# RWKV-7 time mixing in a two-layer decoder trunk: the keys as three split products, the gate's low-rank input mixed on VectorE

## The chip, the cores and the metric

The kernel runs on one core of a Trainium2 chip, in one launch. The metric is the device time of one execution in microseconds (us), as the median of several. A core has TensorE (PE; its weight loads are listed apart as PEld), VectorE (DVE), ScalarE (ACT), GpSimd (POOL) and SyncE (SP, which issues the loads here). Each engine works through a queue of its own in order, and waits for the others by semaphores.

## The reference, cut to what matters

The trunk has two layers over 256 tokens of width 1024. The first mixes tokens by RWKV-7 time mixing, the second by windowed attention; each layer has a half-step SwiGLU feed-forward net before and after the mixing. The change lies in the front of time mixing, where the projections are made:

```python
def rwkv7_time_mix(x, mu, w_rkv, w_o, w0, w1, w2, a0, a1, a2, g1, g2, ...):
    x_prev = jnp.pad(x, ((0, 0), (1, 0), (0, 0)))[:, :-1]
    xx = x_prev - x
    xr, xw, xk, xv, xa, xg = [x + xx * mu[i] for i in range(6)]
    r = xr @ w_rkv[0]
    k = xk @ w_rkv[1]                       # 256x1024 by 1024x1024
    v = xv @ w_rkv[2]
    w = -softplus(-(w0 + jnp.tanh(xw @ w1) @ w2)) - 0.5
    a = sigmoid(a0 + (xa @ a1) @ a2)
    g = sigmoid(xg @ g1) @ g2               # g1: 1024x128
    ...                                     # recurrence over tokens, normalization by head
    return (y * g) @ w_o
```

## The kernel before, in words

Everything is in float32, with tiles of 128 partitions; a width of 1024 is 8 chunks of 128 (KT), the tokens are two halves of 128 (`toks`). A float32 matmul takes two PE records for each call. Most of the large products avoid that: `mm3` (L180) and the feed-forward nets (L298, L299) split both operands into a high part, rounded to fp32r, and the low rest, and add three fp32r products, each one record: high by high, high by low, low by high. ACT casts the high part of a weight (L158, L141, `split` at L268), DVE subtracts for the low part (L164, L142, L269).

The front of time mixing does not split. In the order of the program it is:

- `tm_consts` (L442): during the feed-forward net ahead, loads the low-rank weights `lora1` and multiplies them by mu on DVE (L447), once for each of w1, a1 and g1, so that xw @ w1 = u @ w1 + xx @ (mu w1).
- `tm_in(i)` (L468), for each half of the tokens: normalizes, transposes (L263), scales into `uT` (ACT L479, DVE L482) and makes the difference `xx` (L488).
- `mix` (L459): u + xx mu for one of the inputs, 8 instructions on DVE (L456).
- `tm_lora(i)` (L509): 32 calls of 128x128x128 for one half, u and xx against both halves of `lora1` (L516); then tanh, copy and sigmoid on ACT (L518 to L520).
- `v_half` (L544): one half of tokens by 512 columns of w_v (L551).
- in `tm_core`: decay and gate of the low-rank inputs (L580, L586, L581, L588), cumulative decay by a matmul with a triangle (L595) and its exponentials on ACT into `Dp` and `Di` (L598, L599).
- K, in four steps p of 256 output columns: `k_mm(p)` (L637, by `feat_raw`) loads two raw weights of 128x1024 and issues 16 float32 matmuls of 256 columns (L506); `k_norm` squares, sums by head and scales (ACT L647, L649, L659, L661; PE L654; DVE L665, L666), `k_fin` transposes back (PE L677). `k_mm(1)` comes between `k_norm(0)` and `k_fin(0)`, and so on (L711 to L730). R follows the same way, by `feat_raw` (L690).

Raw weights lie in a pool of four buffers (`wr`), so a load on SP's queue (L123) starts when the user of the buffer four earlier is through. PSUM banks for these products are four.

Behind this come the inverses and the recurrence, in two halves of heads (`hh`) and two blocks of 64 tokens by halves. Its last part, where this document looks: `u_step` (L846 matmuls, L847 copies), `x_step` (L855 matmuls, L856 on DVE), what the state of the block before takes from the right-hand side `xtl` (L951 matmuls, L952 on DVE), the output sums (L865, L876), the normalization by head `gn_half` (L964 to L990, DVE L984 and L985), and `out_proj` (L994) with w_o split by L141 and L142, the transposed output by L268 and L269.

The order on each engine isn't the order of the code: the whole program is scheduled before it is built, from estimated durations, and the sequence for each engine's queue is fixed then. A change in one stage can so move instructions in another. The code's own dependences for order (`after`, `gate`, `behind`) hold in both versions.

Of the kernel before, what the change touches and what calls it, by code (L numbers as in the profile page):

```python
# [9 lines left out]
F32R = mybir.dt.float32r  # L10
AF = mybir.ActivationFunctionType
ALU = mybir.AluOpType
# [4 lines left out]
P = 128  # L17
D = 1024
T = 256
KT = 8  # L20
# [29 lines left out]
class Trunk:  # L50
# [129 lines left out]
    def mm3(self, out, l, r, first, last):  # L180
        mm = self.nc.tensor.matmul
# [259 lines left out]

    def tm_consts(self):  # L442
        nc = self.nc
        u, x = self.l1 = [self.tl("l1", [P, KT, 256], tag=f"l1{j}") for j in range(2)]
        self.load(u, self.a["lora1"].rearrange("p (k c) -> p k c", k=KT), self.mid)
        for j, c0, cw in ((1, 0, 64), (4, 64, 64), (5, 128, 128)):
            nc.vector.tensor_tensor(x[:, :, c0:c0 + cw], u[:, :, c0:c0 + cw],  # L447
                                    self.cols[:, C_MU + j * 8:C_MU + j * 8 + 8].unsqueeze(2).to_broadcast([P, KT, cw]),
                                    op=ALU.mult)
        nc.gpsimd.memset(self.hwa[64:65, 0, :], 1.0)  # L450
        nc.gpsimd.memset(self.hwa[0:64, 1, :], 0.0)
        nc.gpsimd.memset(self.hwa[0:1, 1, :], 1.0)
# [56 lines left out]
    def tm_lora(self, i):  # L509
        nc = self.nc  # L510
        sl = slice(i * P, (i + 1) * P)
        bs = [self.bank()[:, 0:P] for _ in range(2)]
        for e, (l, x) in enumerate(zip(self.l1, (self.uT, self.xx))):
            for j in range(2):
                for k in range(KT):
                    nc.tensor.matmul(bs[j], l[:, k, j * P:(j + 1) * P], x[:, k, sl], start=(k == 0 and not e),  # L516
                                     stop=(k == KT - 1 and e == 1))
        nc.scalar.activation(self.hwa[0:64, 0, sl], bs[0][0:64, :], AF.Tanh)  # L518
        nc.scalar.copy(self.hwa[64:128, 1, sl], bs[0][64:128, :])
        nc.scalar.activation(self.sgT[:, sl], bs[1], AF.Sigmoid)  # L520

    def tm_core(self):
        nc, a, DC = self.nc, self.a, self.DC
        mm = nc.tensor.matmul
        TT, STT = nc.vector.tensor_tensor, nc.vector.scalar_tensor_tensor
# [5 lines left out]
        toks = [slice(0, P), slice(P, T)]  # L531
# [5 lines left out]
        nc.vector.tensor_scalar(self.ka1, self.cols[:, C_KA:C_KA + KT], -1.0, 1.0, op0=ALU.mult, op1=ALU.add)  # L537
        nc.vector.tensor_scalar(self.nkk, self.cols[:, C_KK:C_KK + KT], -1.0, None, op0=ALU.mult)
        xv = self.tl("xt", [P, KT, P], tag="xv0")
        xk = self.tl("xt", [P, KT, T], tag="xtl")  # L540
        self.mix(xv, 3, toks[0])
        self.mix(xk[:, :, toks[0]], 2, toks[0])
        self.tm_lora(0)
        def v_half(n, x):  # L544
            acc = self.bank()
            ns = slice(n * 512, n * 512 + 512)
            for k2 in range(4):
                w = self.pp.tile([P, 2, 512], F32, name=f"wr{self.uid()}", tag="wr", bufs=4)
                self.load(w, a["w_v"][2 * k2:2 * k2 + 2, :, ns].rearrange("k p c -> p k c"))
                for k in range(2):  # L550
                    mm(acc, x[:, 2 * k2 + k, :], w[:, k, :], start=(k2 + k == 0), stop=(k2 + k == 4))  # L551
            return acc

        acc0 = v_half(0, xv)
        self.mix(xk[:, :, toks[1]], 2, toks[1])
        self.tm_lora(1)
        self.close("g2k", "t4", "W1", "W2", "l1")
        self.banks(4, 2)
# [1 line left out]
        self.open("GS")  # L560
        self.open("pk")
        self.open("ar", side="right")
        pk = lambda tag, shape, bufs=1: self.pools["pk"].tile(shape, F32, name=f"{tag}_{self.uid()}", tag=tag, bufs=bufs)
        vv = self.tl("el", [P, 2, D], tag="vv")
        v0 = vv[:, 0, 0:512]
# [9 lines left out]
        for i in range(2):  # L575
            sw.append(pk("p1", [P, D], 2))
            for n in range(2):
                ns = slice(n * 512, n * 512 + 512)
                b = self.bank()
                mm(b, self.hwa[0:65, 0, toks[i]], l2[0][0:65, ns], start=True, stop=True)  # L580
# [9 lines left out]
        for n in range(2):  # L590
            for i in range(2):
                b = self.bank()
# [12 lines left out]
        f = lambda ap: ap.rearrange("p s t -> p (s t)")  # L605
# [29 lines left out]
        kst = {}  # L635

        def k_mm(p):  # L637
            kst[p] = [self.feat_raw(a["w_k"], p, xk)]

        def k_norm(p):  # L640
            kb = kst[p][0]
# [158 lines left out]
        for s in range(31):  # L800
            n = 31 - s
# [20 lines left out]
        for hh in range(2):  # L822
            b = self.cbank()
            for v in range(16):
                for e in range(2):
                    mm(b[hi[e], v * 32:v * 32 + 32], ga(e, hh)[lo[e], v, 32:64], T1[lo[e], hh * 16 + v, :],
                       start=True, stop=True)
            for e in range(2):
                nc.scalar.copy(M1[hi[e], hh * 16:hh * 16 + 16, :], b[hi[e]].rearrange("p (v t) -> p v t", v=16))
        for hh in range(2):  # L830
            b = self.cbank()
            for v in range(16):
                for e in range(2):
                    mm(b[lo[e], v * 32:v * 32 + 32], M1[hi[e], hh * 16 + v, :], Wd[hi[e], hh * 16 + v, :],
                       start=True, stop=True)
# [62 lines left out]
        for e in range(2):  # L898
            for mq in range(2):
                b = self.tbank()  # L900
# [25 lines left out]
        y = [yy[:, 0], yy[:, 1]]  # L926
# [17 lines left out]
        for hh in range(2):  # L944
            s = slice(hh * 64, hh * 64 + 64)
            b = self.cbank()
# [365 lines left out]
```

## Time and profile before

| what | us |
|---|---|
| median of 3 runs | 1119.68 (1118.95 to 1120.72) |
| the profiled execution | 1121.3 |
| its span, first to last instruction | 1119.5 |
| PE busy in the span | 1087.2 (97%) |
| DVE busy | 684.0 (61%) |
| ACT busy | 547.1 (49%) |
| POOL busy | 66.5 (6%) |

So 1.8 us lie around the span, and the profiled execution is 1.6 us above the median. The granted clock of PE had a mean of 0.977 of full speed.

How to read the lines: in the timeline a row has the start, the duration, the engine, the line of the kernel, the operation, output and inputs by the program's names, the shape and, behind an x, how many instructions of a kind are merged; a bracket gives the idle time ahead of it and who ended it. PE's records overlap: a record is longer than the distance to the next one, so the rate is read from starts. In the table of windows a row has the stretch, its length, the busy time and count of PE, PEld, DVE, ACT and POOL, the granted clock, the busy share of the DMA engines and GB/s. In the groups by line, behind the bar stand the total busy time and the mean ns of one.

### The profile page before, as it was taken

The numbers are of one execution on the slowest core, as the hardware profiler recorded it, in microseconds if no ns is written. First come the engines' busy times: TensorE is split into PE (matmuls) and PEld (weight loads), VectorE is DVE, ScalarE is ACT, GpSimd is POOL, SyncE is SP. The second block draws the span as 40 slices with busy tenths as digits, with TensorE's granted clock in tenths as the row PEclk, the third lists the DMA queues.
The fourth block names the chain that finished last, engine by engine and source line by source line (L and its number), as shares of the span: only waits on it lengthen the run. The fifth ranks groups of instructions, "written<-read, shape, count | busy, mean of one in ns | idle before, by whom it ended". The sixth has DMA issues, their size and how long they took to land.

```text
span 1119.5 us, 16276 instructions
## 1 busy us (share of the span) xinstructions
PE 1087.2 (97%) x6360; PEld 895.8 (80%) x6360; DVE 684.0 (61%) x1076; ACT 547.1 (49%) x972; POOL 66.5 (6%) x68
## 2 busy tenths in 40 slices
PE   7999999999999999999999899999999899999997
PEld 5888888778777787888888678888887567888886
DVE  6666664615581677776565767656647756766652
ACT  6554553263322235665554546555535655655541
POOL 0000000000000000000000600000022421000000
PEclk9999999999987699999999999999999899999999
DMA  8767662223442332677665356665624324766521
GB/s 287 227 194 272 221 190 97 95 71 99 133 132 89 117 99 94 227 242 234 200 190 162 117 166 236 185 246 189 190 88 152 131 94 134 262 204 191 189 93 38
DMA packets 52957, 184.10 MB, mean 164 GB/s; under 512 B 5776, under 2 KB 6032, under 8 KB 52752
## 3 DMA queue, kind: packets, MB, share of 16 engines
q1 hardware_dynamic: 52592, 182.53, 50.1%
q8 instruction: 50, 0.82, 0.3%
q10 hardware_dynamic: 288, 0.52, 0.1%
q14 instruction: 27, 0.22, 0.1%
HBM read 181.98 MB, written 1.05 MB: 163 GB/s over the span
## 4 chain that ended last, share of the span: by engine, by line
PE 87%; issue 4%; DVE 4%; ACT 2%; DMA 2%; POOL 1%; SPq 0%; POOLq 0%; DVEq 0%; ACTq 0%
PE bt L298 12%; PE bk L298 12%; PE bk L182 11%; PE bk L186 11%; PE bk L187 11%; PE bk L299 6%; PE bt L299 6%; PE bk L506 5%; PE bk L551 3%; PE bt L616 2%; POOL W L162 1%; PE bt L625 1%; PE bt L263 1%; PE bc L846 1%; PE bk L876 1%
## 5 line engine op out<-in xcount | busy, mean ns | idle before, releaser
L164 DVE TENSOR_TENSOR W<-wr,W 128x1024 fp32r<-128x1024 f32 x267 | 327.9, 1234 | 192.3 <-ACT W L158 190.8
L158 ACT CAST W<-wr 128x1024 fp32r<-128x1024 f32 x284 | 296.3, 1050 | 210.7 <-issue 98.9
L186 PE MATMUL bk<-W,g2k 128*128 128x512 f32 x352 | 138.6, 394 | 0.0
L182 PE MATMUL bk<-W,g2k 128*128 128x512 f32 x352 | 138.5, 395 | 0.0
L187 PE MATMUL bk<-W,g2k 128*128 128x512 f32 x352 | 138.3, 394 | 0.0
L298 PE MATMUL bk<-xtl,W 128*128 128x512 f32 x296 | 105.2, 395 | 0.0
L298 PE MATMUL bt<-xtl,W 128*128 128x512 f32 x296 | 104.9, 394 | 0.0
L298 PE MATMUL bt<-xth,W 128*128 128x512 f32 x296 | 104.8, 393 | 0.0
L298 PE MATMUL bk<-xth,W 128*128 128x512 f32 x296 | 104.8, 393 | 0.0
L299 PE MATMUL bt<-xth,W 128*128 128x256 f32 x296 | 82.9, 280 | 0.0
L299 PE MATMUL bk<-xtl,W 128*128 128x256 f32 x296 | 82.9, 280 | 0.0
L299 PE MATMUL bt<-xtl,W 128*128 128x256 f32 x296 | 82.9, 281 | 0.0
L299 PE MATMUL bk<-xth,W 128*128 128x256 f32 x296 | 82.9, 280 | 0.0
L182 PEld LDWEIGHTS bk<-W,g2k 128*128 128x128 f32 x352 | 66.1, 188 | 15.6
L187 PEld LDWEIGHTS bk<-W,g2k 128*128 128x128 f32 x352 | 66.0, 188 | 15.7
L186 PEld LDWEIGHTS bk<-W,g2k 128*128 128x128 f32 x352 | 66.2, 188 | 14.2
L162 POOL TENSOR_TENSOR W<-wr,W 128x512 fp32r<-128x512 f32 x34 | 48.8, 1462 | 356.1 <-ACT W L158 356.1
L298 PEld LDWEIGHTS bk<-xth,W 128*128 128x128 f32 x296 | 55.6, 188 | 12.6
L298 PEld LDWEIGHTS bt<-xtl,W 128*128 128x128 f32 x296 | 55.6, 188 | 12.6
L298 PEld LDWEIGHTS bk<-xtl,W 128*128 128x128 f32 x296 | 55.6, 188 | 12.5
L298 PEld LDWEIGHTS bt<-xth,W 128*128 128x128 f32 x296 | 55.5, 188 | 12.5
L299 PEld LDWEIGHTS bk<-xtl,W 128*128 128x128 f32 x296 | 55.8, 188 | 1.3
(274 smaller groups left out, 1792.6 us busy)
## 6 DMA issues: line engine op xcount, KB each, us to landing
wr<-in_w_in_dram SPq DMA_DIRECT2D x148, 512.0 KB, 3.8
wr<-in_w_out_dram SPq DMA_DIRECT2D x88, 512.0 KB, 3.6
wr<-in_w_in_lead_dram SPq DMA_DIRECT2D x28, 512.0 KB, 3.9
wr<-in_w_v_dram SPq DMA_DIRECT2D x16, 512.0 KB, 3.9
gain<-in_rows_dram SPq DMA_DIRECT2D x15, 512.0 KB, 5.5
wr<-in_w_k_dram SPq DMA_DIRECT2D x8, 512.0 KB, 4.2
wr<-in_w_r_dram SPq DMA_DIRECT2D x8, 512.0 KB, 3.5
wr<-in_w_o_dram SPq DMA_DIRECT2D x8, 512.0 KB, 3.8
```

Of the source, the lines that this page charges most:

```text
L158: self.follow(nc.scalar.copy(w[:, 0, :], raw), 0)
L162: self.follow(nc.gpsimd.tensor_tensor(w[:, 1, ns], raw[:, ns], w[:, 0, ns], op=ALU.subtract), 2)
L164: self.follow(nc.vector.tensor_tensor(w[:, 1, :], raw, w[:, 0, :], op=ALU.subtract), 1)
L182: m = mm(out, l[0], r[0], start=first, stop=False)
L186: mm(out, l[0], r[1], start=False, stop=False)
L187: return mm(out, l[1], r[0], start=False, stop=last)
L263: t = self.nc.tensor.transpose(b[:, k * P:(k + 1) * P], xn[:, c:c + P], self.ident)
L298: mm(banks[j], hi[:, c0:c0 + P], xt[c][:, :, k4, :], start=(k == 0), stop=False)
L299: use[0] = mm(banks[j][:, 0:T], lo[:, c0:c0 + P], xt[c][:, 0, k4, :], start=False, stop=(k == KT - 1))
L506: mm(b[:, j * T:(j + 1) * T], ws[k // 4][:, c0:c0 + P], xf[:, k, :], start=(k == 0), stop=(k == KT - 1))
L551: mm(acc, x[:, 2 * k2 + k, :], w[:, k, :], start=(k2 + k == 0), stop=(k2 + k == 4))
L616: mm(bb[hh][:, (2 * x + sl) * N:(2 * x + sl + 1) * N], l, r, start=True, stop=True)
```

## The change

**The gate's low-rank input.** DVE mixes xg = u + xx mu (8 instructions for each half, into a tile of the pool `l1`), and `tm_lora` multiplies it once by g1: 8 calls fewer for each half. The product mu g1 in `tm_consts` goes.

**The keys.** The mixed xk goes to another tile, is cast to fp32r by ACT and its rest is made by DVE, for each half of the tokens. `k_mm` splits each raw weight in two halves of 512 columns (ACT L268, DVE L269) into one of three buffers of the new pool `kw`, and issues `mm3` of 256 columns: 48 products for each p, 192 in all, where 64 float32 calls with two records each were.

```diff
-        for j, c0, cw in ((1, 0, 64), (4, 64, 64), (5, 128, 128)):
+        for j, c0, cw in ((1, 0, 64), (4, 64, 64)):
...
         for e, (l, x) in enumerate(zip(self.l1, (self.uT, self.xx))):
-            for j in range(2):
-                for k in range(KT):
-                    nc.tensor.matmul(bs[j], l[:, k, j * P:(j + 1) * P], x[:, k, sl], start=(k == 0 and not e),
-                                     stop=(k == KT - 1 and e == 1))
+            for k in range(KT):
+                nc.tensor.matmul(bs[0], l[:, k, 0:P], x[:, k, sl], start=(k == 0 and not e),
+                                 stop=(k == KT - 1 and e == 1))
+        for k in range(KT):
+            nc.tensor.matmul(bs[1], self.l1[0][:, k, P:2 * P], self.xg[:, k, :], start=(k == 0), stop=(k == KT - 1))
...
-        xk = self.tl("xt", [P, KT, T], tag="xtl")
+        xkm = self.tl("xt", [P, KT, T], tag="xth")
+        xkh = self.tl("xt", [P, KT, T], F32R, tag="xtl")
+        def mix_g(i):
+            self.xg = self.tl("l1", [P, KT, P], tag="xg")
+            self.mix(self.xg, 5, toks[i])
+
+        mix_g(0)
         self.mix(xv, 3, toks[0])
-        self.mix(xk[:, :, toks[0]], 2, toks[0])
+        self.mix(xkm[:, :, toks[0]], 2, toks[0])
         self.tm_lora(0)
...
+        mix_g(1)
...
+        self.open("kw")
+        kw = lambda tag, shape, bufs: self.pools["kw"].tile(shape, F32R, name=f"{tag}_{self.uid()}", tag=tag, bufs=bufs)
+        xk = kw("xkl", [P, KT, T], 1)
+        for i in range(2):
+            self.nc.scalar.copy(xkh[:, :, toks[i]], xkm[:, :, toks[i]])
+            TT(xk[:, :, toks[i]], xkm[:, :, toks[i]], xkh[:, :, toks[i]], op=ALU.subtract)
...
         def k_mm(p):
-            kst[p] = [self.feat_raw(a["w_k"], p, xk)]
+            b = self.bank()
+            for c in range(2):
+                raw = self.raw(a["w_k"][2 * p + c])
+                for n in range(2):
+                    w = kw("wk", [P, 2, 512], 3)
+                    ns = slice(n * 512, n * 512 + 512)
+                    self.split(w[:, 0], w[:, 1], raw[:, ns])
+                    for j in range(2):
+                        for k2 in range(2):
+                            k = 4 * c + 2 * n + k2
+                            c0 = k2 * 256 + j * P
+                            self.mm3(b[:, j * T:(j + 1) * T], (w[:, 0, c0:c0 + P], w[:, 1, c0:c0 + P]),
+                                     (xkh[:, k, :], xk[:, k, :]), k + j == 0, k == KT - 1, skip_group_check=True)
+            kst[p] = [b]
...
-        self.close("pk")
+        self.close("kw", "pk")
```

The new code has 27 lines more by the end of `k_mm`, so the lines behind it are numbered higher: L647 becomes L674, L665 L692, L846 L873, L856 L883, L952 L979, L985 L1012. Between, L580 becomes L594, L595 L609, L598 L612, L762 L789.

**Where instructions moved.** Three places matter below. The first is ACT's queue between the low-rank products of the first half of tokens and those of the second, with the copies of `tm_in` for the second half (L479). `sgT` is the gate, `vv` the values, `wk` a half chunk of split keys' weights. Before:

```order
L519 COPY hwa<-bk_1799 64x128
L520 ACT_TABLE_LOAD
L520 ACTIVATE sgT<-bk_1800 128x128
L479 ACTIVATE u_94<-bt_1755,cols 128x128
L479 ACTIVATE u_94<-bt_1765,cols 128x128
L566 COPY vv_1926<-bk_1836 128x512
L479 ACTIVATE u_94<-bt_1755,cols 128x128
L479 ACTIVATE u_94<-bt_1765,cols 128x128
```

With the change:

```order
L520 COPY hwa<-bk_1808 64x128
L268 CAST wk_2014<-wr_2012 128x512
L521 ACT_TABLE_LOAD
L521 ACTIVATE sgT<-bk_1809 128x128
L268 CAST wk_2029<-wr_2012 128x512
L575 CAST xtl_1782<-xth_1781 128x8x128
L479 ACTIVATE u_94<-bt_1754,cols 128x128
L268 CAST wk_2046<-wr_2044 128x512
L479 ACTIVATE u_94<-bt_1764,cols 128x128
L479 ACTIVATE u_94<-bt_1754,cols 128x128
L580 COPY vv_1936<-bk_1837 128x512
L479 ACTIVATE u_94<-bt_1764,cols 128x128
```

Three casts of keys' weights, the first of which waits for its load, and the cast of the first half of xk now stand among the copies.

The second place is ACT's queue ahead of the exponentials. `p` are sigmoids of the decay, `av` those of the low-rank a, and L762 (L789) copies a part of `vv` whose mix stands late on DVE. Before:

```order
L581 ACTIVATE p_295_1935<-bk_1939 128x512
L762 COPY u_2421<-vv_1926 64x2x4x64
L762 COPY xx_2422<-vv_1926 64x2x4x64
L581 ACTIVATE p_298_1942<-bk_1943 128x512
L581 ACTIVATE p_298_1942<-bk_1946 128x512
L588 ACTIVATE av_1952<-bk_1949 128x512
L661 ACTIVATE p_321_2023<-av_1952,ka_77,cols 128x256 x2
L588 ACTIVATE av_1957<-bk_1954 128x512
L588 ACTIVATE av_1962<-bk_1959 128x512
L588 ACTIVATE av_1967<-bk_1964 128x512
L598 ACT_TABLE_LOAD
```

With the change:

```order
L595 ACTIVATE p_303_1952<-bk_1956 128x512
L602 ACTIVATE av_1962<-bk_1959 128x512
L688 ACTIVATE p_330_2077<-av_1962,ka_77,cols 128x256 x2
L602 ACTIVATE av_1967<-bk_1964 128x512
L789 COPY u_2608<-vv_1936 64x2x4x64
L789 COPY xx_2609<-vv_1936 64x2x4x64
L602 ACTIVATE av_1972<-bk_1969 128x512
L602 ACTIVATE av_1977<-bk_1974 128x512
L612 ACT_TABLE_LOAD
```

The two copies of `vv` moved from behind the second sigmoid to a place ahead of the last two, nearer to the table load.

The third place is DVE's queue at the end of the recurrence, in stages that the diff doesn't touch. `xtl` is the right-hand side that the products of `u_step` read, `xth` the output under normalization, `wo` the split output weight, `BK` the split output. Before:

```order
L984 TENSOR_TENSOR xth_3131<-xth_3131,gst_3390 128x8x64 x2
L952 TENSOR_TENSOR xtl_2427<-xtl_2427,bc_3244 128x8x64
L985 TENSOR_TENSOR xth_3131<-xth_3131 128x8x64 x2
L952 TENSOR_TENSOR xtl_2427<-xtl_2427,bc_3262 128x8x64
L142 TENSOR_TENSOR wo_3374<-wr_3375,wo_3374 128x1024
```

With the change:

```order
L1011 TENSOR_TENSOR xth_3318<-xth_3318,gst_3577 128x8x64 x2
L1012 TENSOR_TENSOR xth_3318<-xth_3318 128x8x64 x2
L979 TENSOR_TENSOR xtl_2614<-xtl_2614,bc_3431 128x8x64
L979 TENSOR_TENSOR xtl_2614<-xtl_2614,bc_3449 128x8x64
L142 TENSOR_TENSOR wo_3561<-wr_3562,wo_3561 128x1024
```

The first subtraction from `xtl` now stands behind both additions of L985 (now L1012). On ACT at the same place, one copy of `u_step` moved ahead of the casts of w_o; before:

```order
L982 ACTIVATE gst_3390<-gst_3390 128x8 x2
L141 CAST wo_3374<-wr_3375 128x1024
L141 CAST wo_3374<-wr_3379 128x1024
L847 COPY u_2421<-bc_3280 64x8x64
L268 CAST BK_3385<-bt_3414 128x4x128
```

With the change:

```order
L1009 ACTIVATE gst_3577<-gst_3577 128x8 x2
L874 COPY u_2608<-bc_3467 64x8x64
L141 CAST wo_3561<-wr_3562 128x1024
L141 CAST wo_3561<-wr_3566 128x1024
L874 COPY u_2608<-bc_3477 64x8x64
L268 CAST BK_3572<-bt_3601 128x4x128
```

The copy waits for products (L873) that read `xtl` after the first subtraction, so the casts behind it wait for them too.

More of the change, by code (lines that the diff above doesn't have):

```diff
@@ L178, in follow, with mm3 @@
             self.tc.add_manual_dep(ins.ins, self.behind[e], GATE, reason="order of the splits")
-    def mm3(self, out, l, r, first, last):
-        mm = self.nc.tensor.matmul
+    def mm3(self, out, l, r, first, last, **kw):
+        mm = lambda *x, **y: self.nc.tensor.matmul(*x, **y, **kw)
         m = mm(out, l[0], r[0], start=first, stop=False)
@@ L443, in tm_consts @@
         nc = self.nc
-        u, x = self.l1 = [self.tl("l1", [P, KT, 256], tag=f"l1{j}") for j in range(2)]
+        u, x = self.l1 = [self.tl("l1", [P, KT, 256 - 128 * j], tag=f"l1{j}") for j in range(2)]
         self.load(u, self.a["lora1"].rearrange("p (k c) -> p k c", k=KT), self.mid)
-        for j, c0, cw in ((1, 0, 64), (4, 64, 64), (5, 128, 128)):
+        for j, c0, cw in ((1, 0, 64), (4, 64, 64)):
             nc.vector.tensor_tensor(x[:, :, c0:c0 + cw], u[:, :, c0:c0 + cw],
@@ L554, in tm_core @@
         acc0 = v_half(0, xv)
-        self.mix(xk[:, :, toks[1]], 2, toks[1])
+        mix_g(1)
+        self.mix(xkm[:, :, toks[1]], 2, toks[1])
         self.tm_lora(1)
```

## The prediction

> **What bounds the kernel now.** I read the chain that ended last first, then the busy times by stretch of the front of time mixing (199 to 225 us the low-rank inputs, to 235 the gates, to 300 the keys and what follows).
>
> ```profile
> PE 87%; issue 4%; DVE 4%; ACT 2%; DMA 2%; POOL 1%; SPq 0%; POOLq 0%; DVEq 0%; ACTq 0%
> ```
> ```profile
> 199.00:225.00 26.00, 24.79 (x163) 19.59 (x162) 17.90 (x55) 8.12 (x24) 1.25 (x3) 1.00 0.31 102
> 225.00:235.00 10.00, 10.00 (x56) 7.82 (x54) 2.28 (x9) 8.73 (x15) 0.00 (x0) 1.00 0.16 52
> 235.00:300.00 65.00, 64.17 (x462) 52.80 (x462) 27.87 (x52) 24.41 (x55) 0.00 (x0) 1.00 0.37 114
> ```
>
> TensorE carries 87% of the chain. From 235 us on it is busy 64.2 of 65 us while VectorE and ScalarE have more than half of their time free: products removed there are time removed. The first two stretches look as full but aren't bound by PE: ScalarE has 8.7 of 10 us between 225 and 235, and the rows below show PE's starts hanging on copies and exponentials.
>
> **The front, up to the first key product.** PE's starts, then VectorE's, ScalarE's, and two prices from the page:
>
> ```profile
> 209.02 7.03 PE L551 MATMUL bk<-wr,xv 128*128 128x512 f32 x16
> ...
> 216.94 4.13 PE L516 MATMUL bk<-u,l 128*128 128x128 f32 x32
> 220.91 3.74 PE L516 MATMUL bk<-xx,l 128*128 128x128 f32 x32
> 224.48 3.60 PE L580 MATMUL bk<-gain,hwa 65*128 65x512 f32 x8
> ...
> 235.24 7.17 PE L506 MATMUL bk<-xtl,wr 128*128 128x256 f32 x32
> ```
> ```profile
> 204.63 1.13 DVE L456 SCALAR_TENSOR_TENSOR xv<-xx,cols,u 128x128 f32<-128x128 f32 x4
> ...
> 216.93 0.79 DVE L482 TENSOR_SCALAR u<-bt,cols 128x128 f32<-128x128 f32 x2 [7.21 <-ACT u L479]
> 218.11 0.61 DVE L482 TENSOR_SCALAR u<-bt,cols 128x128 f32<-128x128 f32 x2 [0.39 <-ACT u L479]
> ...
> 225.37 1.92 DVE L456 SCALAR_TENSOR_TENSOR vv<-xx,cols,u 128x128 f32<-128x128 f32 x7
> ```
> ```profile
> 209.73 0.28 ACT L520 ACTIVATE sgT<-bk 128x128 f32<-128x128 f32 x1
> 216.52 0.81 ACT L479 ACTIVATE u<-bt,cols 128x128 f32<-128x128 f32 x2 [6.51 <-PE bt L263]
> ...
> 232.81 1.28 ACT L598 ACT_TABLE_LOAD   x1
> ...
> 234.60 0.59 ACT L599 ACTIVATE Di<-bk 128x512 f32<-128x512 f32 x1
> ```
> ```profile
> L164 DVE TENSOR_TENSOR W<-wr,W 128x1024 fp32r<-128x1024 f32 x267 | 327.9, 1234 | 192.3 <-ACT W L158 190.8
> L158 ACT CAST W<-wr 128x1024 fp32r<-128x1024 f32 x284 | 296.3, 1050 | 210.7 <-issue 98.9
> ...
> wr<-in_w_k_dram SPq DMA_DIRECT2D x8, 512.0 KB, 4.2
> ```
>
> *The low-rank products.* 16 records fewer for each half, 32 in all, at 3.74/32 = 0.117 us: 3.74 us of PE. I book nothing for it. For the first half, PE waits afterwards for u of the second (u at 216.9); for the second, the 8 calls by xg must wait until VectorE has mixed it. The mix is 8 x 0.263 (1.05 us from one row's start to the next for four) = 2.1 us in each half, ahead of the other mixes. The multiplication of g1 that goes lies in the feed-forward net ahead, where it hid already.
>
> *What ScalarE and VectorE get more.* Two casts of xk (1.05 each) and two rests (1.23), and 16 half casts (0.53) and rests (0.62) of keys' weights. Three of the casts and one of xk stand among the copies of u. Their weight is loaded when `v_half` frees a buffer, after its second matmul: it starts some 1.9 before its old 209.0 (16 records fewer) and has four records at 0.44 (7.03/16) by then, so the load starts at 209 and lands 4.2 later, at 213. Then come cast 0.53 (half of 1.05, as a rest is half of 1.23), table load 1.28, gate 0.28, cast 0.53, cast of xk 1.05: the copy of u starts at 216.7, where it started at 216.5. On VectorE the rest of xk (1.23) stands ahead of the scaling of u, so it starts at 217.9 instead of 216.9, and the third cast stretches what follows: u is complete at 220.25 instead of 218.72 (1.5 late). xg is there at 225.1, and the decay (L580, now L594) starts at 225.45 instead of 224.48.
>
> *Up to the keys.* The last mixes end at 227.29 before (225.37 + 1.92). Added ahead of them are 1.5 of lateness, 2.1 of xg and 1.23 of the second rest of xk, less 0.4 of gaps that fill: 231.7. The copies of `vv` (L789) wait for these mixes, and in ScalarE's new order two sigmoids and the table load wait behind the copies: 231.85 + 1.24 for the copies + 1.0 for the sigmoids = 234.1, where the table load began at 232.81. The first product of K needs the bank that L599 reads last, so it follows that: 234.60 + 0.59 = 235.19 against the start at 235.24. Now it starts 1.25 later, at 236.5. **Term: +1.25**; from 0, if the copies are ready earlier, to +2.5, if the load of w_k lands a microsecond later and all stands behind it.
>
> **The keys.** A PE record of 512 and one of 256 columns in turn, from a feed-forward net, the weight loads of the second kind, the start of the second `v_half` behind K and R(0), and three prices of what stands between the casts:
>
> ```profile
> 104.22 0.40 PE L298 MATMUL bk<-xtl,W 128*128 128x512 f32 x1
> 104.45 0.28 PE L299 MATMUL bk<-xtl,W 128*128 128x256 f32 x1
> 104.58 0.39 PE L298 MATMUL bk<-xtl,W 128*128 128x512 f32 x1
> ...
> 107.00 0.39 PE L298 MATMUL bk<-xth,W 128*128 128x512 f32 x1
> ```
> ```profile
> L299 PEld LDWEIGHTS bk<-xtl,W 128*128 128x128 f32 x296 | 55.8, 188 | 1.3
> ```
> ```profile
> 284.66 0.65 PE L677 MATMUL bk<-cst,p 128*128 128x128 f32 x4
> 285.15 5.32 PE L551 MATMUL bk<-wr,xv 128*128 128x512 f32 x12
> ```
> ```profile
> L659 ACT ACTIVATE p<-rr 128x512 f32<-128x512 f32 x4 | 2.5, 628 | 18.0 <-DVE rr L657 18.0
> L661 ACT ACTIVATE p<-av,ka,cols 128x256 f32<-128x256 f32 x6 | 3.2, 586 | 0.0
> ```
>
> Before, K is 128 records at 7.17/32 = 0.224: 28.7 us. Now it is 192 products of 256 columns. Eight pairs of 512 and 256 take 107.00 - 104.22 = 2.78, 0.347 each; less 0.23 (104.22 to 104.45) leaves 0.117 for 256 columns. 192 x 0.117 = 22.5: **term -6.3**.
>
> No row shows 256-column fp32r passes alone, each with a new weight. The low bound is 0.117, as the float32 records of 128 columns above also come, a new weight each, at 0.117. The high bound is the 0.188 of a load's record, as if loads could not overlap: 36.1 us, +7.4. I take 0.117, since 0.347 for two passes is already less than two loads of 0.188. Beside it, the Trainium skill, page "TensorE: Matmul & The Clock Gate", section "The mechanism" of its Part 3, states that a weight load overlaps running matmuls only if its row group differs, and section "LDWEIGHTS (loading the stationary operand)" gives columns/1.2 ns, 107 ns for 128. By it I estimate 192 x (0.107 + 0.117) = 43 us, 14 more than K has now; the measured pair of 0.347 is below the 0.56 it would need, so the trace speaks against it.
>
> *Do the splits keep up?* A half chunk is 12 products, 1.40 us; its cast and rest, 0.53 and 0.62 on two engines, fit. The queue matters: three buffers let ScalarE run ahead by two half chunks, and in K(1) the ninth cast waits for the products of the sixth; behind it stand a table load (1.28), L659 (0.63) and two L661 (1.17), then the tenth cast (0.53) and its rest (0.62), 4.8 us with the ninth itself, in which PE has three half chunks, 4.2, and transposes of 0.5 (284.66 to 285.15). That leaves 0.1; VectorE, though, is then at products of k_norm and k_fin over 512 columns (0.68, as L952 below), of which two can stand ahead of the rest. I take 1.2 of idle PE there. **Term: +1.2**, from 0.1 to 2.5. The later steps have the table loaded and no such row. So the second `v_half` starts at 285.15 + 1.25 - 6.3 + 1.2 = 281.3.
>
> **The end of the recurrence.** The inverses and most of the recurrence keep their order. Not so at 405 us:
>
> ```profile
> 406.53 0.68 DVE L952 TENSOR_TENSOR xtl<-xtl,bc 128x512 f32<-128x512 f32 x1
> 407.13 1.29 DVE L985 TENSOR_TENSOR xth<-xth 128x512 f32<-128x512 f32 x2
> ...
> 408.93 2.35 DVE L142 TENSOR_TENSOR wo<-wr,wo 128x1024 fp32r<-128x1024 f32 x2
> 411.20 1.28 DVE L269 TENSOR_TENSOR BK<-bt,BK 128x512 fp32r<-128x512 f32 x2
> 412.40 1.31 DVE L856 TENSOR_TENSOR xtl<-xtl,bc 64x512 f32<-64x512 f32 x2
> ```
> ```profile
> 407.26 1.14 PE L846 MATMUL bc<-xtl,W 64*64 64x64 f32 x16 [0.36 <-DVE xtl L952]
> ...
> 414.96 1.14 PE L846 MATMUL bc<-xtl,W 64*64 64x64 f32 x16
> ```
> ```profile
> 406.94 1.99 ACT L141 CAST wo<-wr 128x1024 fp32r<-128x1024 f32 x2 [1.77 <-PE bk L865]
> 408.96 0.58 ACT L847 COPY u<-bc 64x512 f32<-64x512 f32 x1
> ```
>
> L952 now stands behind both L985, 1.2 later, so the products L846 that wait for it (407.26) start near 408.5 and end near 409.6. The copy of u, now ahead of the casts of w_o, ends at 410.25; there the casts start instead of 406.94. VectorE works in order: its two rests of w_o (1.18 each) follow the casts, 411.25 to 413.6, then L269 to 414.85, and only then L856, 2.45 later than 412.40. The second L846 behind it (414.96) runs about 2.05 later, 0.4 being lost in products that can go ahead. Afterwards the products are in one row with no slack up to out_proj. **Term: +2.05**, from 0 (the queues meet otherwise) to 2.45.
>
> **Sum**: 1.25 - 6.3 + 1.2 + 2.05 = -1.8. Against its own execution 1121.3 - 1.8 = 1119.5; the median lies 1.6 below that, so 1119.7 - 1.8 = **1117.9**. All else keeps its order.
>
> **Rivals.**
> *B, the end costs nothing*: if the front shifts so that L952 and the casts meet as before, -3.85 stays, 1115.8. For it: such collisions depend on tenths of a microsecond. Against: VectorE's order is fixed, and the casts stand behind the copy.
> *C, ScalarE's queue holds K more often*: with idle as in K(1) in each of the other three steps, +3.6, 1121.5; the same if the front takes its upper bound as well, 1122.8, just slower. For it: ScalarE has 24.4 of 65 us before, and 16 casts add 8.5. Against: half of it is still free.
> *D, the weight load sets the pace of the products* (the other side): 0.188 a product, +13.6 on the sum, 1131.5. It decides from 0.150 a product (28.7/192), where K's gain is gone. For it: load records of 188 ns. Against: the pair of 0.347.
> *E, the clock*:
>
> ```profile
> 372.00:388.00 16.00, 15.28 (x89) 12.37 (x88) 11.85 (x16) 4.54 (x7) 0.00 (x0) 0.50 0.30 99
> 403.00:404.00 1.00, 0.00 (x0) 0.00 (x0) 1.00 (x2) 0.00 (x0) 0.00 (x0) 1.00 0.00 0
> ```
>
> A sparse stretch (89 records in 16 us) ran at half clock, while one idle microsecond did nothing. The front loses 16 records between 216 and 225 and gets idle time; if PE's clock is halved there for some 3.4 us, or one such stretch later grows by as much, half of it is lost, +1.7: 1119.6. The Trainium skill, same page, section "What's actually happening", states such a window of 3.4 us; the clock column of before agrees in that half clock comes after sparse stretches.
>
> **How the numbers follow.** A measurement of this kernel can tell about 0.2%, 2.2 us, from no change. My forecast has 50% (1116.7 to 1119.2; a fifth of it beyond the bound on the fast side), B 26%, C 11%, D 5%, E 8%. Faster: 0.26 + 0.11 = 0.37. Slower: D and half of C, 0.11. Between: 0.52. The range leaves out D, the dearest third of C and the lower part of B: 1115.0 to 1121.2.
>
> **What would show it.** Right: the first key product near 236.5, keys' records at 0.117, one idle of about 1.2 in K(1), the second `v_half` near 281.3, and the last L873 2 us later against the start of that stage. Wrong: key records over 0.15 apart; gaps in each step; or the casts of w_o at the old distance from L865.

## The result and the profile after

| | kernel before | with the change |
|---|---|---|
| median | 1118.95 us (11 runs, 1116.91 to 1121.58) | 1124.47 us (11 runs, 1120.3 to 1128.12) |
| ratio | | 1.0053 (1.0041 to 1.0066) |
| the profiled execution | 1121.3 us, span 1119.5 | 1120.3 us, span 1118.5 |
| its granted clock | 0.977 | 0.978 |

The change makes the kernel 0.5% slower, outside the predicted range. The profiled execution of the changed kernel was the fastest of its eleven, and that of before, with 1121.3 us, lies above ten of its eleven, so the two traces show 1 us the other way. They still show where things moved. First TensorE (PE) from the first key product on:

```profile
236.27 0.39 PE L181 MATMUL bk<-xtl,wk 128*128 128x256 f32 x1 [0.78 <-ACT Di L613]
236.49 0.28 PE L181 MATMUL bk<-xkl,wk 128*128 128x256 f32 x1
236.61 0.40 PE L181 MATMUL bk<-xtl,wk 128*128 128x256 f32 x2
236.85 0.28 PE L181 MATMUL bk<-xkl,wk 128*128 128x256 f32 x1
...
249.58 0.60 PE L704 MATMUL bk<-cst,p 128*128 128x128 f32 x4
251.37 0.38 PE L681 MATMUL bk<-cst,p 128*128 128x2 f32 x2 [1.20 <-ACT p L674]
...
263.48 1.10 PE L639 MATMUL bt<-AR,BH 64*128 64x64 f32 x8
264.51 0.39 PE L181 MATMUL bk<-xkl,wk 128*128 128x256 f32 x1
...
284.25 7.03 PE L558 MATMUL bk<-wr,xv 128*128 128x512 f32 x16
```

The first product stands 1.03 later than before (235.24), three products come every 0.36 us (236.49 to 236.85), there is one wait of 1.20 behind the second step's products (ahead of L681), and the second `v_half` starts only 0.9 earlier than at 285.15. Then the end of the recurrence, on ScalarE, VectorE and PE:

```profile
408.26 0.58 ACT L874 COPY u<-bc 64x512 f32<-64x512 f32 x1 [4.47 <-PE bc L873]
408.86 1.99 ACT L141 CAST wo<-wr 128x1024 fp32r<-128x1024 f32 x2
```
```profile
406.35 1.27 DVE L979 TENSOR_TENSOR xtl<-xtl,bc 128x512 f32<-128x512 f32 x2
409.94 2.36 DVE L142 TENSOR_TENSOR wo<-wr,wo 128x1024 fp32r<-128x1024 f32 x2 [2.32 <-ACT wo L141]
412.22 1.28 DVE L269 TENSOR_TENSOR BK<-bt,BK 128x512 fp32r<-128x512 f32 x2
413.42 1.26 DVE L883 TENSOR_TENSOR xtl<-xtl,bc 64x512 f32<-64x512 f32 x2
```
```profile
400.40 0.27 PE L977 MATMUL bc<-c,AR 64*64 64x64 f32 x2 [0.91 <-DVE c L968]
402.80 0.27 PE L978 MATMUL bc<-c,AR 64*64 64x64 f32 x1 [1.23 <-DVE c L969]
...
414.14 1.14 PE L873 MATMUL bc<-xtl,W 64*64 64x64 f32 x16 [0.85 <-DVE xtl L883]
...
431.33 1.03 PE L263 MATMUL bt<-cst,xth 128*128 128x128 f32 x8
```

The casts of w_o wait for the copy, VectorE has 2.32 of idle time, L883 comes late, and PE waits for it at 414. The waits of 0.9 and 1.2 ahead of the state's products (L977 and L978, which were L950 and L951) are there in the kernel before as well:

```profile
401.79 0.27 PE L950 MATMUL bc<-c,AR 64*64 64x64 f32 x2 [0.92 <-DVE c L941]
404.18 0.27 PE L951 MATMUL bc<-c,AR 64*64 64x64 f32 x1 [1.23 <-DVE c L942]
```

What the durations don't show stands in the column of the granted clock. Three fences show the same stretches (the second copies of u in the front, then the end of the recurrence as a whole): of before, of the change, and of a second trace of the changed kernel (the first experiment):

```profile
215.50:219.00 3.50, 3.46 (x25) 2.74 (x24) 1.59 (x5) 1.74 (x5) 0.00 (x0) 1.00 0.94 324
219.00:222.50 3.50, 3.50 (x34) 3.50 (x33) 3.50 (x11) 0.00 (x0) 0.00 (x0) 1.00 0.10 39
...
400.00:421.00 21.00, 18.43 (x363) 16.64 (x360) 15.42 (x28) 7.52 (x13) 0.00 (x0) 1.00 0.26 80
```
```profile
215.50:219.00 3.50, 1.93 (x11) 1.45 (x12) 3.21 (x7) 2.51 (x7) 0.00 (x0) 1.00 0.65 208
219.00:222.50 3.50, 3.50 (x19) 3.50 (x18) 3.50 (x13) 0.00 (x0) 0.00 (x0) 0.51 0.60 243
...
400.00:421.00 21.00, 18.19 (x332) 16.58 (x333) 13.49 (x24) 6.13 (x11) 0.00 (x0) 0.92 0.21 77
```
```profile
219.00:222.50 3.50, 3.50 (x20) 3.50 (x19) 3.50 (x12) 0.00 (x0) 0.00 (x0) 0.55 0.66 266
...
400.00:421.00 21.00, 18.80 (x280) 17.30 (x282) 12.77 (x22) 6.27 (x12) 0.00 (x0) 0.67 0.23 77
```

Before had the full clock in all three. With the change a sparse stretch in the front (1.93 of 3.50 us busy) is followed by one at half clock; and of the 21 us at the end of the recurrence 3.4 us ran at half clock in the first trace (2 x 0.08 x 21) and 13.9 in the second (2 x 0.33 x 21), which is four times 3.41.

### The profile page after: what moved, and what is told of

It reads as the page before. It is cut to its first block, busy times and chain, and to the rows that moved or that the text cites. A ratio compares the mean times of both kernels' runs of the same rounds, so it can differ in the third digit from the quotient of the medians.

```text
span 1118.5 us, 16400 instructions
## 1 busy us (share of the span) xinstructions
PE 1080.6 (97%) x6392; PEld 895.3 (80%) x6392; DVE 697.1 (62%) x1109; ACT 557.7 (50%) x990; POOL 65.2 (6%) x68
## 4 chain that ended last, share of the span: by engine, by line
PE 88%; issue 4%; DVE 3%; ACT 3%; DMA 1%; POOL 1%; SPq 0%; DVEq 0%; POOLq 0%; ACTq 0%
PE bk L181 34%; PE bk L298 12%; PE bt L298 12%; PE bk L299 6%; PE bt L299 6%; PE bk L506 3%; PE bk L558 2%; PE bt L630 2%; PE bt L639 1%; POOL W L162 1%; PE bt L263 1%; PE bk L1150 1%; PE bc L873 1%; PE bk L903 1%; PE bk L515 1%
## 5 line engine op out<-in xcount | busy, mean ns | idle before, releaser
L181 PE MATMUL bk<-W,g2k 128*128 128x512 f32 x1056 | 251.5, 395 | 0.0
L181 PEld LDWEIGHTS bk<-W,g2k 128*128 128x128 f32 x1056 | 195.8, 188 | 45.5
L298 PEld LDWEIGHTS bk<-xth,W 128*128 128x128 f32 x296 | 55.6, 188 | 12.6
L298 PEld LDWEIGHTS bt<-xtl,W 128*128 128x128 f32 x296 | 55.6, 188 | 12.6
L298 PEld LDWEIGHTS bt<-xth,W 128*128 128x128 f32 x296 | 55.5, 188 | 12.5
L181 PE MATMUL bk<-W,xtl 128*128 128x512 f32 x216 | 57.0, 409 | 0.8 <-ACT xtl L268 0.6
L299 PEld LDWEIGHTS bt<-xtl,W 128*128 128x128 f32 x296 | 55.7, 188 | 0.2
L299 PEld LDWEIGHTS bt<-xth,W 128*128 128x128 f32 x296 | 55.7, 188 | 0.1
L299 PEld LDWEIGHTS bk<-xth,W 128*128 128x128 f32 x296 | 55.7, 188 | 0.0
```

Of the source, the lines that this page charges most:

```text
L181: mm = lambda *x, **y: self.nc.tensor.matmul(*x, **y, **kw)
L298: mm(banks[j], hi[:, c0:c0 + P], xt[c][:, :, k4, :], start=(k == 0), stop=False)
L299: use[0] = mm(banks[j][:, 0:T], lo[:, c0:c0 + P], xt[c][:, 0, k4, :], start=False, stop=(k == KT - 1))
```

## The experiments

In the table, the ratio is that of timed runs against the kernel before on the same chip; the clock is the mean of these runs, that of the kernel before beside them is 0.980 to 0.982; "400 to 421" is the granted clock there in the one trace of each.

| experiment | ratio (interval) | clock | 400 to 421 |
|---|---|---|---|
| e1, the change again | 1.0065 (1.0046 to 1.0084) | 0.971 | 0.67 |
| e2, the keys only | 1.0056 (1.0043 to 1.0070) | 0.975 | 0.84 |
| e3, the gate only | 1.0067 (1.0050 to 1.0084) | 0.973 | 0.76 |
| e4, filler in the front | 1.0053 (1.0038 to 1.0068) | 0.975 | 0.86 |
| e6, old order at the end | 0.9995 (0.9986 to 1.0005) | 0.980 | 1.00 |
| e7, filler at the end | 1.0001 (0.9991 to 1.0011) | 0.981 | 1.00 |
| e8, before, subtraction moved | 1.0000 (0.9991 to 1.0010) | 0.981 | 0.92 |
| e9, VectorE's part of the old order | 1.0069 (1.0053 to 1.0084) | 0.971 | 0.67 |
| e10, ScalarE's part of the old order | 1.0014 (1.0001 to 1.0027) | 0.979 | 0.92 |
| e11, keys only, old order | 1.0012 (0.9998 to 1.0027) | 0.978 | 1.00 |
| e12, gate only, old order | 1.0046 (1.0025 to 1.0066) | 0.974 | 0.76 |
| e13, e12 and filler at the end | 1.0011 (1.0000 to 1.0021) | 0.980 | 1.00 |
| e14, e11 and filler at the end | 1.0006 (0.9993 to 1.0018) | 0.979 | 1.00 |
| e15, before and filler at the end | 0.9999 (0.9988 to 1.0010) | 0.982 | 1.00 |
| e16, e6 and filler at the end | 1.0001 (0.9990 to 1.0011) | 0.981 | 1.00 |

**e1**, no edit.

> The changed kernel unchanged, for a second trace and more timed runs beside the kernel before. Theory C1 (clock): the trace of the changed kernel has its 6 us not in waits (the output projection's transposes start 0.9 us later than before, 431.33 against 430.44) but in half-clock windows of 3.4 us that fall on sparse stretches of PE, in other places from run to run; then the ratio is 1.004 to 1.007 again, the mean granted clock of the timed runs lies 0.002 to 0.006 below that of the kernel before, and time and clock go together (0.01 of clock about 8 us). Theory C2 (queues): the loss is waits of PE for ScalarE and VectorE in the keys and at the end of the recurrence, the same in each run; then the clock is that of before and the ratio comes without it.

The clock is lower by 0.011, and time goes with it: over the 271 executions whose clock is on record the correlation is -0.93, 7.1 us for 0.01 of clock. The first eleven runs of the change have a mean clock of 0.9733, the 114 of before in the experiments 0.9806; 0.0073 x 710 = 5.2 us of the 5.9 between their means. This is C1 as to the kind, with about twice the fall in clock that it named. A correlation doesn't say which of the two drives the other; the experiments with filler below do. The places were open.

**e2, e3, e4**: one half of the change each, and the change with PE's work put back into the front.

```diff
 # e4, in tm_lora
+        if i:
+            for n in range(2):
+                for k in range(KT):
+                    nc.tensor.matmul(bs[1], self.l1[0][:, k, P:2 * P], self.uT[:, k, 0:P], start=(k == 0), stop=(k == KT - 1))
         for k in range(KT):
             nc.tensor.matmul(bs[1], self.l1[0][:, k, P:2 * P], self.xg[:, k, :], start=(k == 0), stop=(k == KT - 1))
```

> Only the keys as split products; the gate's input by u and mu g1 as before (32 records more in the front than the change has). C1: the front keeps its work, so no half-clock window at 216 to 224; what the keys leave (idle in their second step, the end of the recurrence) costs 0 to 3 us against before, ratio 1.000 to 1.003. C2: the loss lies in the keys and the end, so nearly all of it stays, 1.004 to 1.006.

> Only the gate's input mixed on VectorE; the keys as float32 products as before. C1: the front is sparse, a half-clock window comes at 216 to 224 in part of the runs, ratio 1.001 to 1.004. C2: 0 to 2 us for the later mixes and the end of the recurrence, whose order moves here too, with the clock of before: 1.000 to 1.002.

> The change with 32 records more on PE in the sparse stretch of the front: 16 products of the first half's u by g1 into the gate's bank, whose sum the real products then replace. They depend on nothing that is late; nothing else moves but two rows on VectorE. C1: no half-clock window follows 216 to 220, so 1 to 2 us are gained against the changed kernel in the mean although work is added, ratio 1.002 to 1.005. C2: added work gains nothing: the ratio of the changed kernel or up to 2 us more, 1.005 to 1.007.

Each half carries the whole loss, so it is no sum of two costs; e2 has the time that C2 named, but with a lower clock, which C2 excludes; e3 (1.0067) lies above both theories. e4 gains nothing that the intervals tell, but its filler puts the second `v_half` at 286.96, 2.7 behind the change's, so a gain in the clock could hide behind the added work. It is e2 that shows that the loss doesn't need the front: its trace has full clock there (1.00 from 215.5 to 222.5), and the whole loss. What the three have in common with the change is the scheduler's new order at the end of the recurrence, and half clock there.

**e5 to e8**: the kernel before for a second trace, the old order put back, idle products in PE's two waits at 400, and the new place of the subtraction in the kernel before.

```diff
 # e6: both parts of the old order
-            TT(XV[:, vs(1, hh), :], XV[:, vs(1, hh), :], bm(b), op=ALU.add)
-        u_step(1, 0)
+            xv_upd = TT(XV[:, vs(1, hh), :], XV[:, vs(1, hh), :], bm(b), op=ALU.add)
+            if not hh:
+                xv_first = xv_upd
         y1 = y_open(1, S)
-        x_step(1)
-        u_step(1, 1)
         wp = self.pools["ar"].tile([P, 2, 2, D], F32R, name="wo67", tag="AR")
         wo_early(6, None, None, wp[:, 0])
         wo_early(7, None, None, wp[:, 1])
+        u_step(1, 0)
+        x_step(1)
+        u_step(1, 1)
...
-                TT(d, d, v(hd(B), hh), op=ALU.add)
+                t = TT(d, d, v(hd(B), hh), op=ALU.add)
+                if not i and not hh:
+                    self.tc.add_manual_dep(t.ins, xv_first.ins.name, GATE, reason="order of the tail")
 # e7: products that nobody reads, ahead of L977 and L978
+        def fill(ms):
+            t = self.tbank()
+            for m in ms:
+                for hh in range(2):
+                    o = t[hh * 64:hh * 64 + 64, m * N:(m + 1) * N]
+                    for e in range(2):
+                        mm(o, BKt[:, e, m, hh * 64:hh * 64 + 64], UV[e][:, hh * 16 + 2 * m, :],
+                           start=(e == 0), stop=(e == 1))
+        fill(range(4))
...
         y1 = y_open(1, S)
+        fill(range(5))
...
 # e8: the kernel before
+                if not i and hh:
+                    self.tc.add_manual_dep(xv_first.ins, t.ins.name, GATE, reason="order of the tail")
```

> The kernel before, for a second trace. In the first four experiments the three variants and the changed kernel each had 2 to 4 half-clock windows of 3.4 us between 403 and 421 us, at the end of the recurrence, and 1 ahead of 207 us; the first trace of the kernel before has none in either place. Theory T1 (the end of the recurrence, whose order the scheduler moved in all of them, drops the clock): none or at most one such window between 400 and 420 here too, and 28.6 us from the first product L951 to the transposes of out_proj (401.79 to 430.44). Theory T2 (the windows fall where the phase of the run puts them, for either kernel): windows there in this trace too, as often as not.

> The change with the order of before at the end of the recurrence alone: L979's first subtraction ahead of the second addition of L1012, the casts of w_o ahead of the copy of u. T1: the windows there go, so 4 to 6 us of the loss of 6 to 7 go and the ratio is 0.999 to 1.002, with a clock of 0.978 to 0.982. T2: the order is worth its 2 us of waits, 1.003 to 1.005, and the clock stays near 0.973.

> The change with its own order there, but 36 idle products of the state (nobody reads them) put into PE's two waits of 1.1 and 1.4 us ahead of L977 and L978. If a low load of PE there halves the clock (T1 or T2), the windows between 400 and 420 go although nothing waits less: ratio 1.001 to 1.004, clock over 0.976. If the clock plays no part, the ratio is that of the changed kernel or more, 1.0055 to 1.008.

> The kernel before with nothing of the change, but L952's first subtraction put behind both additions of L985, as the scheduler does in the changed kernel. T1: this alone makes 3 to 6 us, ratio 1.003 to 1.006, with 1 to 4 half-clock windows between 400 and 420 and a clock of 0.975 to 0.979. T2: only the wait of 1 to 2.5 us, ratio 1.001 to 1.002, clock 0.980 to 0.984.

The second trace of before has full clock from 400 to 421 as well, and 28.64 us from the first L950 to out_proj's transposes (28.65 in the first), as T1 said. One thing in that expectation is wrong: e2 has no window ahead of 207. e6 and e7 take the whole loss away. In e6's trace one of the two additions still stands ahead of the first subtraction. e7 has further lines that hold the subtraction behind both additions and the casts behind a copy of u, as in the change; it adds work to PE and takes none away. In its trace the wait of 0.91 ahead of L977 is gone, that of 1.23 ahead of L978 is 0.44, and the clock is full:

```profile
400.00:421.00 21.00, 20.11 (x420) 18.17 (x417) 14.85 (x27) 7.17 (x13) 0.00 (x0) 1.00 0.25 80
```

The half clock goes with the low load, then, and not with the new order as such. In e7 one cast of the split output and four of out_proj's products also start earlier (the products at 410.53, in the change at 418.80), so it isn't the filler alone that differs. e8 speaks against the simple form of T1: the subtraction alone costs nothing, less than either theory said. Its trace has one half-clock window, and then PE is dense (13.00 of 13 us busy from 404 to 417).

**e9, e10**: the two parts of e6 apart.

> The change with only VectorE's part of the old order: L979's first subtraction ahead of the second addition of L1012; ScalarE still copies u ahead of the casts of w_o. Known so far: with both parts of the old order the loss is gone (0.9995), and in the kernel before VectorE's part moved alone costs nothing (1.000), so the two parts aren't alike. Theory U1 (the casts decide: they stand behind a copy that waits for PE, so the rests of w_o and behind them x_step's addition come late and PE stands idle again at 413): the loss stays, 1.004 to 1.007, with 2 to 4 half-clock windows between 400 and 420. Theory U2 (VectorE decides): 0.999 to 1.002.

> The change with only ScalarE's part of the old order: the casts of w_o ahead of the copy of u; VectorE adds twice (L1012) ahead of L979 as in the changed kernel. U1: the loss is gone, 0.999 to 1.002, clock 0.979 to 0.982. U2: it stays, 1.004 to 1.007, clock 0.970 to 0.976.

U1: the casts decide. Their rows on ScalarE in e9 and in e10, with the stretch:

```profile
409.69 0.58 ACT L874 COPY u<-bc 64x512 f32<-64x512 f32 x1 [4.82 <-PE bc L873]
410.54 1.99 ACT L141 CAST wo<-wr 128x1024 fp32r<-128x1024 f32 x2 [0.27 <-PE bk L892]
```
```profile
400.00:421.00 21.00, 18.38 (x274) 16.82 (x271) 13.71 (x24) 6.41 (x11) 0.00 (x0) 0.67 0.25 80
```
```profile
406.89 1.99 ACT L141 CAST wo<-wr 128x1024 fp32r<-128x1024 f32 x2 [3.29 <-PE bk L892]
408.91 1.30 ACT L874 COPY u<-bc 64x512 f32<-64x512 f32 x2
```
```profile
400.00:421.00 21.00, 19.49 (x338) 17.91 (x339) 14.95 (x29) 6.67 (x13) 0.00 (x0) 0.92 0.24 77
```

Both traces drop to half clock behind the waits at 400; with the casts early PE has 338 records in the stretch and is back at full clock after one window, with the casts late 274, and it stays low for four. Two traces alone don't show that the casts make this difference: the changed kernel, with one order, had 332 records and one window in its first trace, 280 and four in its second. For the casts speak the timed runs, with intervals that don't meet (1.0001 to 1.0027 against 1.0053 to 1.0084) and clocks of 0.979 against 0.971.

**e11 to e16**: each half with the old order, both again with the filler (the function above), the filler in the kernel before, and the change with both.

> Only the keys as split products, with the old order at the end of the recurrence. In the first experiment with the keys alone the second v_half began at 282.08 (284.74 and 285.15 in the two traces of before) and the loss lay behind 400. If that loss is the order's, 2 to 3 us are won: ratio 0.997 to 0.999. If the keys carry a loss of their own, 1.001 or more.

> Only the gate's input on VectorE, with the old order at the end of the recurrence. If the loss of the gate alone (1.0067) is the order's, it goes: 0.999 to 1.002, left over being half-clock windows at 203 and 220. If it is the front's clock, 1.003 or more stays.

> The gate's input alone, old order at the end of the recurrence (1.0046 without filler, its trace with three half-clock windows from 407.6), and 36 idle products of the state put into PE's waits around 400. V1 (the clock that drops after the sparse stretch at 400 is what costs, in whatever order): the windows between 400 and 420 go, ratio 0.999 to 1.001, clock 0.979 to 0.983 in each run. V2 (the gate's mixes in the front cost by themselves, and the windows are another sign of it): 1.003 to 1.005.

> The keys alone as split products, old order, and the same filler (1.0012 without it, runs from 1116.4 to 1123.5). V1: the runs draw together at the low end, about 1116 to 1117.5, ratio 0.997 to 0.999, the gain that the second v_half shows (282.11 against 284.74). V2: 1.000 to 1.002.

> The kernel before with the filler alone. Its two traces show no half-clock window at the end of the recurrence. V1: nothing to win there, 0.999 to 1.001. If the kernel before loses time there too in part of its runs, 0.997 to 0.999.

> The whole change with the old order at the end of the recurrence and the filler there, the version that the experiments point to. Without the clock the change is worth about 1 us (second v_half at 284.25 against 284.74 and 285.15, less what remains at the end). V1: ratio 0.998 to 1.000, clock 0.979 to 0.983, no half-clock window between 400 and 420. If another stretch, the front or 306 to 388, takes more windows instead, 1.000 to 1.002.

The order isn't the whole: e12 has it, and still three half-clock windows in its trace and runs from 1117.81 to 1127.79 us. With the filler on top (e13) the loss shrinks from 0.46% to 0.11%, just above V1's range, while the front and the mixes stay as they were; VectorE's order at 409 moves a little with the filler. The same filler does nothing for the kernel before. V1 holds for the loss. It does not hold for the gain: e11, e14 and e16 have full clock there in their traces and are not faster than before. In the trace of e14 the second `v_half` is at 282.95, 2 us ahead of before; the mean clock of its runs is still 0.979, and they go from 1115.78 to 1122.05. Whether other half-clock stretches take this gain was not tried further. For the whole change (e16) a gain of 1 us, as expected, lies inside the interval and can't be told from none.

Whether half clock follows the waits at 400 goes with where they meet a border of the clock's windows. The half-clock stretches of one trace begin and end on one grid of 3.413 us, which can be carried on from the end of the stretch ahead (388.26 us in before, 386.35 in the change, 388.02 in e6, 390.53 in e12). Thirteen traces have no filler at the end. In nine of them the first product of the state (L977, or L950 in before) starts 0.18 to 0.58 or 2.80 to 2.96 us behind a border, and half clock follows; in the other four (both of before, e6, e11) it starts 3.11 to 3.29 or 0.13 us behind one, and none does. PE's busy time ahead of the border doesn't tell the two apart; in each pair of rows, the first of e6, the second of e12, the first row is the window with the longer wait:

```profile
401.68:405.09 3.41, 2.18 (x80) 2.04 (x78) 3.26 (x10) 0.33 (x2) 0.00 (x0) 1.00 0.22 62
405.09:408.50 3.41, 2.32 (x69) 2.18 (x64) 3.38 (x7) 1.84 (x2) 0.00 (x0) 1.00 0.29 96
```
```profile
404.18:407.59 3.41, 2.18 (x79) 2.04 (x77) 3.27 (x10) 0.34 (x2) 0.00 (x0) 1.00 0.34 114
407.59:411.01 3.42, 3.20 (x53) 3.02 (x50) 3.38 (x7) 1.35 (x2) 0.00 (x0) 0.50 0.16 44
```

So the 1.00 of e6 and e11 in the table, one trace each, isn't the order's doing. The filler's is: in e15 and e16 the first product starts 0.38 and 0.32 us behind a border, a place that drops without filler, and the clock stays full (e7, at 0.77, lies where no trace without filler does).

## Why the prediction was wrong, point by point

- **The front, +1.25**: right in size, by another path. The first key product stands at 236.27 (forecast 236.5), +1.03, and the wait in front of it is for `Di` (L613), as said. But the copies of `vv` (L789) didn't wait for the mixes of `vv`, which end at 226.3 and not at 231.7; the table load (233.84, 1.03 late) follows from ScalarE's own queue, in which the second cast of xk (225.26) stands ahead of the first sigmoid. The term left half clock out, and the front is dearer where it falls there: from the last transposes (L263, at 198 to 200 us) to the first key product it is 36.20 us in before, 37.25 in e16 with full clock in the front, 37.68 in the change with the one window at 219, and 39.10 in the second trace with another from 202 to 206.
- **The keys, -6.3**: mis-sized. The pass is 0.120 (0.36/3), not 0.117, and the 192 products with the switches between them take 24.2 us of PE's starts (22.5 forecast), against 28.7 before: -4.5. Rival D, a pace of 0.188, is refuted.
- **Idle in the second step, +1.2**: right in size, 1.20 ahead of L681, and due to the same stretch of ScalarE's queue (cast, table load, L686, L688, cast). The wait that ends last is another: it is for the squares (L674) behind the tenth cast, not for that cast's rest on VectorE. What was missed: the products L639 between the keys' products come 8 in 1.03 us (263.48 to 264.51), where 16 took as long before, +1.3; L630 has +0.3. So from the first key product to `v_half` it is 47.98 us against 49.91, -1.9 instead of -5.1. The waits that rival C expected in the other steps didn't come.
- **The end of the recurrence, +2.05**: the chain of waits was right. L883 stands 13.02 us behind the first L977 (413.42 less 400.40), L856 stood 10.61 behind L950: 2.4 later, the forecast 2.45. That the number fits so well is in part luck, as a half-clock window lies in this stretch; in e7, with the subtraction and the casts in the new order, filler and full clock, it is 12.18, 1.6 later. From the first L977 to the transposes it is 30.93 against 28.65, +2.3, in the first trace; but in the second, with the same waits at 400, 34.40 (435.03 less 400.63), +5.75, while e7 has 28.91. As far as e7 tells, little of the loss there is left at full clock. The row of the transposes in the second trace:

```profile
435.03 1.03 PE L263 MATMUL bt<-cst,xth 128*128 128x128 f32 x8
```

- **The sum**: by the first trace 1.0 - 1.9 - 0.5 + 2.3 = +0.9 at the transposes (431.33 against 430.44), forecast -1.8; by the second +4.6, near the median's 5.5. Two steps failed. One is the price of the end of the recurrence, bounded at 2.45 by durations at full clock, as if a stretch that gets sparser cost only its waits; it measured up to 5.75. The other is the keys' stretch, -1.9 where -5.1 was forecast, mostly through the term of -6.3; with it alone the sum is +1.4 (1.25 - 1.9 + 2.05). The first trace of each kernel hides the first of these: that of before has three half-clock windows behind 879 us (clock 0.50 from 879.8 to 886.6 and from 934.4 to 937.8) that the one of the change doesn't have. In the sum of the chances a fifth of 50% is 0.10, where 0.11 was added; that changes nothing.
- **Rival E** had the mechanism, half clock after a sparse stretch, at 8%, but priced it as one window of 3.4 us and looked for it in the front. The front's window came (219 to 222.5 at 0.51), and one from 202 to 206 in the second trace; restoring work there (e4) did not tell in the time. At the end of the recurrence there were up to four in a row. That they last because what follows is itself sparse in the new order is argued, not shown: one order gave one window and four. The quoted row of before is part of five windows in a row (371.2 to 388.3) and had shown that one window isn't the bound; I read it for its start alone. It also shows that "sparse" isn't idle: PE was busy for 15.28 of its 16 us, and for all 3.41 us ahead of the drop, with products of 64 by 64.

The Trainium skill, page "TensorE: Matmul & The Clock Gate", section "What's actually happening", states windows of 3413 ns that run free of the program, so that one kernel meets them at another phase in each run. The traces agree: half-clock stretches of one to six times 3.41 us, on a grid that lies 2.55 and 1.53 us behind the first instruction in the two traces of before, 0.64 and 0.88 in those of the change. The section "HAM oscillation — how this bites in real kernels" of that page warns of idle gaps above about 3.4 us. Here waits of 0.9 and 1.2 us within 3.4 us did it, with products of 64 by 64 between them; the measurement decides.

What stays open: how long half clock lasts once it has come, one window or four in the changed kernel from the same place on the grid (0.40 and 0.39 us behind a border); and what exactly the gate counts, as busy time doesn't tell. The waits at 400 are the same in all thirteen traces without filler; where a border falls on them differs, and that could not be set in an experiment.

## What to carry to other kernels

Where a change makes the scheduler put instructions in another order far behind it, look for places that wait at low load of PE, and price them with the clock: a stretch of a few waits of 1 us can turn the 3 to 14 us behind it to half clock. Judge by many runs with their clocks, since one trace can show the opposite sign, as here. A cheap test for the clock as a cause is work that nobody reads, put into the waits: here it took back nearly all of a loss of 0.5 to 0.7%.

## What the runs showed of the hardware that was not expected

- After the two waits of 0.92 and 1.23 us at 400 us half clock followed in some executions and not in others of kernels with the same waits there: none in two traces of the kernel before, one window in one and four in the other of the changed kernel. Where the waits lie on the grid of 3.413 us separates all thirteen traces.
- Products of 128x256 in fp32r, each with a new weight, come every 0.120 us, with load records of 189 to 190 ns beside them.
- PE was busy by its records for all of the 3.41 us from 367.8 to 371.2 in the kernel before, with products of 64 by 64, and half clock followed.
- Work added to PE, 36 products that nobody reads, made the gate's half 0.35% faster (1.0046 to 1.0011).
